# 512-column weight units over two row tiles in the second MLP products and the first half of the output projections of a diffusion trunk

## The chip, the cores and the metric

The kernel runs on one core of one Trainium2 chip. The core has TensorE (PE in the profile: matmuls, with a queue of its own for weight loads, PEld), VectorE (DVE), ScalarE (ACT), GpSimd (POOL) and SyncE (SP, which issues the DMAs here). The metric is the device time of one execution in microseconds (us); the figure for a kernel is the median of its runs. The profile comes from one profiled execution, and its times are counted from the start of that execution's span.

## The reference, cut to what matters

One inference step of a trunk of four layers, for 128 context tokens and 512 latent tokens with 1024 features each. Each layer has a token mixer (0 differential attention, 1 neighbourhood attention, 2 grouped-query attention, 3 a Hyena long convolution) and a squared-ReLU MLP, each with a residual, a LayerNorm and a modulation by a vector of conditions:

```python
for i in range(DEPTH):                                   # 4 layers
    mod_p = jnp.split((silu_ctx @ ada_w[i] + ada_b[i])[:, None, :], 6, axis=-1)
    mod_s = jnp.split((silu_c @ ada_w[i] + ada_b[i])[:, None, :], 6, axis=-1)
    hp, hs = modulate(xp, mod_p[0], mod_p[1]), modulate(xs, mod_s[0], mod_s[1])
    op, os_ = ...                                        # the mixer; its last step is  o @ w_o
    xp = layer_norm(DN_ALPHA * xp + mod_p[2] * op, ln_g[i, 0], ln_b[i, 0])
    xs = layer_norm(DN_ALPHA * xs + mod_s[2] * os_, ln_g[i, 0], ln_b[i, 0])
    fp = squared_relu_mlp(modulate(xp, mod_p[3], mod_p[4]), mlp_w1[i], mlp_w2[i])
    fs = squared_relu_mlp(modulate(xs, mod_s[3], mod_s[4]), mlp_w1[i], mlp_w2[i])
    xp = layer_norm(DN_ALPHA * xp + mod_p[5] * fp, ln_g[i, 1], ln_b[i, 1])
    xs = layer_norm(DN_ALPHA * xs + mod_s[5] * fs, ln_g[i, 1], ln_b[i, 1])

def squared_relu_mlp(h, w1, w2):                         # w1: 1024 x 4096, w2: 4096 x 1024
    return jnp.square(jax.nn.relu(h @ w1)) @ w2
```

The change concerns two products: `... @ w2` in the MLPs of layers 1, 2 and 3, and `o @ w_o` at the end of each mixer.

## The kernel before, in words

**Precision and tiles.** The 640 tokens are five row tiles of 128 (`NT` = 5; tile 0 is the context). Every product is made in split precision: each operand is held as a rounded part and a remainder, and `mm3` (L473) issues three matmuls for one product of 128x128 by some columns, at L475, L476 and L477. In the MLP's second product and in the output projection the 128x128 operand loaded into TensorE is an activation (`ff`, `oh`), and the columns streamed past it are those of a weight unit.

**Weight units.** Weights come from memory in units of 128x1024 elements, 512 KB, in the order of one list that `weight_order` (L346) writes. SP loads a unit into one of three `raw` buffers; `w_convert` (L436) makes the two parts of it in one of five `hl` buffers: a cast on ScalarE (L451), then a subtraction on VectorE (L453). `wget` (L463) hands the next unit of the list to the code and converts two more ahead (one, where `ahead=1`). A unit before the change (`unit_b`) holds four row blocks of the weight (the inner dimension, 4 x 128) by 256 columns.

**The MLP** (`mlp`, L864) runs through eight chunks of 512 inner features. For a chunk it makes the first product (`w1_unit`, 320 columns a matmul, rows with `hh` and `hl` as inputs), then the second product of the chunk before: four units `q`, and for each of them five row tiles in `w2_group` (L909), 12 matmuls of 256 columns into one PSUM tile named `w`. The tile comes from `any1` (L337), which takes four PSUM buffers in turn. Chunk 7's second product is made in `sublayer_end` and stays as it is.

**Evacuation.** `residual` (L649) takes the result off: a multiply by a gate on VectorE (L655, `gtmp`, three buffers) and an addition to the residual `r` (L662), on VectorE or GpSimd in a fixed ratio.

**Side work.** Between units `side` (L1543) works off what stands next in the list: steps of the next layer's modulation (adaLN; on VectorE, L543, with two loads on SP each, `adaw`), and in layers 0 to 2 the filters and their spectra for the Hyena mixer, whose DFT tables (`hyt`) stay in `hl` buffers while they are in use.

**The output projection** (`out_steps`, L825) has two halves of the inner dimension. The first half is a generator: 20 groups (four units by five tiles) that the mixer's end takes as filling work, each yield telling how much TensorE work it was; `out_rest` (L848) runs it down to 6 groups, prepares the second half in between, and takes the rest. `out_left` counts. The second half stays as it is.

Of the kernel before, what the change touches and what calls it, by code (L numbers as in the profile page):

```python
# [18 lines left out]
P = 128  # L19
# [10 lines left out]
DEPTH = 4  # L30
# [13 lines left out]
AHD = 1  # L44
OL0 = 20
OL1 = 6
WS = (0, 1, 2)
# [9 lines left out]
TSTEP = 3  # L57
LT = 3
CT = 4

# [138 lines left out]


def prepare(inp):
    g = {n: np.asarray(a) for n, a in inp.items()}
# [13 lines left out]
    d["w1"] = np.stack([np.stack([unit_a(g["mlp_w1"][l], np.arange(f * P, f * P + P)) for f in range(32)]) for l in range(DEPTH)])  # L216
    d["w2"] = np.stack([np.stack([unit_b(g["mlp_w2"][l], 4 * ch, q * 256) for ch in range(8) for q in range(4)]) for l in range(DEPTH)])
    for nm, wq, cf in (("da", g["da_w_qkv"][0], da_cols), ("na", g["na_w_qkv"][0], na_cols)):
# [7 lines left out]
    for nm, wo in (("da", g["da_w_o"][0]), ("na", g["na_w_o"][0]), ("gq", g["gq_w_o"][0][rows]), ("hy", g["hy_w_o"][0])):  # L226
        d[nm + "_o"] = np.stack([unit_b(wo, 4 * kh, q * 256) for kh in range(2) for q in range(4)])
    ck = g["cache_da_k"][0, 0].reshape(P, D)
# [51 lines left out]
class Trunk:  # L280
# [65 lines left out]
    def weight_order(self):  # L346
        out = []
        for n, l in enumerate(self.layers):
# [16 lines left out]
            for ch in range(9):  # L365
                for i in range(8):
                    if (ch < 8) if i < 4 else (ch > 0):
                        out.append(("w1", l, 4 * ch + i) if i < 4 else ("w2", l, 4 * ch + i - 8))
                        if 0 < ch < 8:
                            out += ada[:1] + side[i // 4].get(4 * (ch - 1) + i % 4, [])  # L370
                            ada = ada[1:]
        return out
# [270 lines left out]
    def restore(self):  # L643

        f, self.fetch_r = self.fetch_r, None
        if f:
            f()

    def residual(self, ps, t, q, quick=False):  # L649

# [169 lines left out]
    def out_first(self, l, nm, split):  # L820

        self.out_left = 4 * NT
        return self.out_steps(l, nm, split)

    def out_steps(self, l, nm, split):  # L825
        self.restore()
        self.load_gates(l, 0, (0,))
        gate = self.gate
        oh = self.out_half()
        self.w_convert(self.wi + 1)  # L830
        split(oh, 0, 0)
        split(oh, 0, 1)
        yield 1
        for q in range(4):
            u = {q: self.wget((nm + "_o", q), ahead=1)}
            if q == 1:
                self.load_gates(l, 0, (1,))
                gate.update(self.gate)
                self.gate = gate
            for t in range(NT):  # L840
                if q == 0 and t + 2 < NT:
                    split(oh, 0, t + 2)
                self.out_group(u, oh, t, (q,))
                self.out_left -= 1
                yield 1280
        self.scale_r = False

    def out_rest(self, l, nm, split, first):  # L848
        self.share = QW
        self.load_ln(l, 0)  # L850
        while self.out_left > 6:
            next(first)
# [11 lines left out]
    def mlp(self, l, nxt, last):  # L864
# [52 lines left out]
        for ch in range(8):  # L917
# [7 lines left out]
            for f in range(4):  # L925
                w1_unit(4 * ch + f)
                self.side()
            for q in range(4):
                u = self.wget(("w2", l, 4 * (ch - 1) + q))
                for t in range(NT):  # L930
                    w2_group(u, ch - 1, q, t)
                    groups += 1
                    if self.taps and groups % TSTEP == 0:
                        self.tap_step()
                self.side()
# [606 lines left out]

    def side(self):  # L1543

        while self.wlist[self.wi][0] in ("ada", "hyw", "hyt", "hyd", "hyc"):
            key = self.wlist[self.wi]
# [411 lines left out]
class Feeder:  # L1958
# [29 lines left out]
    def close(self):  # L1988
# [5 lines left out]
        self.debt += CRATE  # L1994
        while self.debt > 0 and self.k.out_left > 6:
            self.debt -= next(self.first)
# [237 lines left out]
```

## Time and profile before

| | us |
|---|---|
| median of three runs (lowest, highest) | 3492.54 (3490.21, 3494.48) |
| the profiled execution | 3491.57 |
| its span in the trace | 3489.7 |
| TensorE busy, 25288 matmuls | 3320.7 (95%) |
| TensorE's weight loads | 3187.3 (91%) |
| VectorE | 2603.5 (75%) |
| ScalarE | 1511.8 (43%) |
| GpSimd | 1010.7 (29%) |

In the chain of work that ended last TensorE has 57% of the span and VectorE 14%. The MLPs of layers 1, 2 and 3 lie at about 1300 to 1785, 2130 to 2617 and 3014 to 3480 us, the ends of the mixers, where the output projections run, at 337 to 444, 1208 to 1279, 2019 to 2116 and 2930 to 3001 us. Two things help in reading. Matmuls are pipelined, so the duration of one (0.28 us for 256 columns) overlaps the next; the rate is read from the distance between starts. And names in the trace leave the buffer's number out: `w` is the PSUM tile of an MLP product, `wo` that of an output projection, `hl` and `ff` are what it reads.

### The profile page before, as it was taken

How to read it: one execution, taken by the hardware profiler on the slowest of the kernel's cores; microseconds unless marked ns; L12 is line 12 of the kernel's file. 1: busy time of each engine (PE TensorE's matmuls, PEld its weight loads, DVE VectorE, ACT ScalarE, POOL GpSimd, SP SyncE). 2: the span in 40 equal slices, each digit the busy share in tenths (PEclk: the TensorE clock that was granted, in tenths of full speed). 3: DMA queues.
4: the chain of work that ended last, by engine and by line, in shares of the span. 5: the costliest groups of instructions: out<-in, count | busy, mean ns of one | idle time of the engine just before them, and what ended most of it. 6: DMA issues, size and time to landing. Idle time of an engine off the chain costs nothing.

```text
span 3489.7 us, 63708 instructions
## 1 busy us (share of the span) xinstructions
PE 3320.7 (95%) x25288; PEld 3187.3 (91%) x25288; DVE 2603.5 (75%) x4691; ACT 1511.8 (43%) x2700; POOL 1010.7 (29%) x961
## 2 busy tenths in 40 slices
PE   8999899999999989999988999999998999999998
PEld 6878899998999989999988889999998998899998
DVE  4777888788586678777677888787759888945457
ACT  4555453333356654433335665333424334432322
POOL 1323333334354453122252014232334112500002
PEclk9999999999999999999999999999999999999999
DMA  7333135545242324556412112545523224232221
GB/s 274 124 128 108 49 128 163 173 162 176 81 131 82 104 76 158 187 168 196 144 60 69 31 53 91 177 162 180 164 96 121 82 75 157 85 94 79 85 75 54
DMA packets 157643, 418.96 MB, mean 120 GB/s; under 512 B 19550, under 2 KB 29414, under 8 KB 154270
## 3 DMA queue, kind: packets, MB, share of 16 engines
q1 hardware_dynamic: 157344, 414.88, 36.3%
q8 instruction: 199, 3.26, 0.4%
q14 instruction: 100, 0.82, 0.1%
HBM read 371.20 MB, written 34.05 MB: 116 GB/s over the span
## 4 chain that ended last, share of the span: by engine, by line
PE 57%; DVE 14%; issue 2%; ACT 2%; DMA 2%; POOL 1%; SPq 0%; DVEq 0%; ACTq 0%; POOLq 0%
PE w L475 12%; PE w L476 12%; PE w L477 12%; DVE hl L453 2%; PE pv L2061 2%; PE s L2014 1%; PE qk L475 1%; PE ptp L1064 1%; DVE ada L543 1%; PE qk L477 1%; PE qk L476 1%; DVE gtmp L655 1%; DVE hl L736 1%; DVE r L662 1%; PE wo L477 1%
## 5 line engine op out<-in xcount | busy, mean ns | idle before, releaser
L662 POOL TENSOR_TENSOR r<-r,gtmp 128x256 f32<-128x256 f32 x444 | 437.7, 999 | 1125.6 <-DVE gtmp L655 1087.7
L453 DVE TENSOR_TENSOR hl<-raw,hl 128x1024 fp32r<-128x1024 f32 x390 | 508.7, 1307 | 317.6 <-ACT hl L451 316.2
L475 PE MATMUL w<-hl,ff 128*128 128x256 f32 x2560 | 715.6, 280 | 7.4 <-DVE gtmp L655 6.9
L476 PE MATMUL w<-hl,ff 128*128 128x256 f32 x2560 | 715.2, 279 | 2.5 <-DVE hl L453 2.4
L477 PE MATMUL w<-hl,ff 128*128 128x256 f32 x2560 | 714.0, 279 | 0.0
L451 ACT CAST hl<-raw 128x1024 fp32r<-128x1024 f32 x411 | 430.1, 1048 | 634.8 <-PE w L477 496.7
L475 PE MATMUL w<-hh,hl 128*128 128x320 f32 (+2 forms) x2048 | 637.2, 311 | 0.2
L476 PE MATMUL w<-hl,hl 128*128 128x320 f32 (+2 forms) x2048 | 634.4, 310 | 2.7 <-DVE hl L736 2.7
L477 PE MATMUL w<-hh,hl 128*128 128x320 f32 (+2 forms) x2048 | 634.0, 310 | 0.0
L475 PEld LDWEIGHTS w<-hl,ff 128*128 128x128 f32 x2560 | 481.2, 188 | 12.1 <-DVE gtmp L655 10.2
L476 PEld LDWEIGHTS w<-hl,ff 128*128 128x128 f32 x2560 | 481.5, 188 | 5.0 <-DVE hl L453 3.3
L477 PEld LDWEIGHTS w<-hl,ff 128*128 128x128 f32 x2560 | 480.3, 188 | 0.0
L543 DVE SCALAR_TENSOR_TENSOR ada<-adaw,sil,ada 128x512 f32<-128x512 f32 x504 | 388.7, 803 | 92.4 <-DMA adaw<-in_ada_w 75.5
L475 PEld LDWEIGHTS w<-hh,hl 128*128 128x128 f32 x2048 | 387.0, 189 | 13.8 <-issue 8.4
L476 PEld LDWEIGHTS w<-hl,hl 128*128 128x128 f32 x2048 | 386.7, 189 | 4.2 <-DVE hl L736 4.2
L477 PEld LDWEIGHTS w<-hh,hl 128*128 128x128 f32 x2048 | 386.5, 189 | 0.8 <-issue 0.8
L655 DVE TENSOR_TENSOR gtmp<-w,gate 128x256 f32<-128x256 f32 x640 | 261.6, 416 | 159.2 <-PE w L477 147.5
L874 ACT ACTIVATE fx<-w 128x640 f32<-128x640 f32 (+2 forms) x136 | 91.5, 672 | 453.8 <-PE w L477 446.4
L475 PE MATMUL qk<-hh,hl 128*128 128x320 f32 (+2 forms) x672 | 216.7, 322 | 6.7 <-DVE gtmp L655 3.9
L476 PE MATMUL qk<-hl,hl 128*128 128x320 f32 (+2 forms) x672 | 211.6, 315 | 1.3 <-DVE hl L736 1.3
L477 PE MATMUL qk<-hh,hl 128*128 128x320 f32 (+2 forms) x672 | 211.5, 315 | 0.0
L475 PE MATMUL wo<-hl,oh 128*128 128x256 f32 x640 | 184.1, 288 | 10.0 <-DVE gtmp L655 5.4
(344 smaller groups left out, 7135.4 us busy)
## 6 DMA issues: line engine op xcount, KB each, us to landing
raw<-in_w SPq DMA_DIRECT2D x256, 512.0 KB
adaw<-in_ada_w SPq DMA_DIRECT2D x288, 256.0 KB
adaw<-in_ada_w SPq DMA_DIRECT2D x16, 1024.0 KB
raw<-ab_d SPq DMA_DIRECT2D x32, 512.0 KB
raw<-in_hy_in SPq DMA_DIRECT2D x24, 512.0 KB
adaw<-in_ada_s SPq DMA_DIRECT2D x8, 1024.0 KB
raw<-in_da_qk SPq DMA_DIRECT2D x16, 512.0 KB
gate<-gate_d SPq DMA_DIRECT2D x32, 256.0 KB
```

Of the source, the lines that this page charges most:

```text
L451: self.nc.scalar.copy(t[:, 0], raw)
L453: sub(t[:, 1], raw, t[:, 0].bitcast(F32))
L475: mm(ps, w[0], x[0], start=start, stop=False)
L476: mm(ps, w[0], x[1], start=False, stop=False)
L477: mm(ps, w[1], x[0], start=False, stop=stop)
L543: nc.vector.scalar_tensor_tensor(out=y, in0=raw[h], scalar=x, in1=y, op0=ALU.mult, op1=ALU.add)
L655: nc.vector.tensor_mul(tmp, ps, self.gate[2 * s + q // 2][:, (q % 2) * 256:(q % 2) * 256 + 256])
L662: eng.tensor_add(rv, rv, tmp)
L736: self.last_dve = sub(self.hl[:, f, c], x, self.hh[:, f, c].bitcast(F32))
L874: nc.scalar.activation(x, src, AF.Relu)
L1064: nc.tensor.transpose(ps[:, i * P:(i + 1) * P], pr[:, (done + i) * P:(done + i + 1) * P], self.ident)
L2061: nc.tensor.matmul(ps[64 * h:64 * h + 64], self.v[:, self.chunk + c, vc:vc + 64], pts[h][:, c * P:(c + 1) * P], start=c == 0, stop=c == se ...
```

## The change

It concerns the second product of chunks 0 to 6 in the MLPs of layers 1 to 3 (`WIDE = 1`: layers from 1 on; the words "MLPs 2 to 4" count from one), and the first half of each of the four output projections.

A unit there is now two row blocks by 512 columns (`unit_w`), of the same 128x1024 elements. Two units make one half of the output columns. `wide_group` makes, for one row tile, 12 matmuls of 512 columns, six from each of the two units, into one PSUM tile of 128x2x256, and then calls `residual` twice, for its two halves of 256 columns. So for each chunk there are two halves by five tiles of wide groups in place of four units by five tiles of narrow ones. The code around it follows: the output projection counts 10 groups in place of 20 (thresholds 3 in place of 6, 2560 in place of 1280 a yield), loads the second half of its gates at the third tile, and takes two units before its first group. `side` is called after the third tile with half of what stands next in the list, and after the fifth with the rest; the list holds side work behind every second unit only.

```diff
-OL0 = 20
-OL1 = 6
+OL0 = 10
+OL1 = 3
+WIDE = 1
+def unit_w(w, k0, c0):
+    return w[k0 * P:(k0 + 2) * P, c0:c0 + 512].reshape(2, P, 512).transpose(1, 0, 2).reshape(P, 1024)
+def units_2(w, k0, wide):
+    if wide:
+        return [unit_w(w, k0 + 2 * kp, h * 512) for h in range(2) for kp in range(2)]
+    return [unit_b(w, k0, q * 256) for q in range(4)]
-    d["w2"] = np.stack([np.stack([unit_b(g["mlp_w2"][l], 4 * ch, q * 256) for ch in range(8) for q in range(4)]) for l in range(DEPTH)])
+    d["w2"] = np.stack([np.stack([u for ch in range(8) for u in units_2(g["mlp_w2"][l], 4 * ch, l >= WIDE and ch < 7)]) for l in range(DEPTH)])
-        d[nm + "_o"] = np.stack([unit_b(wo, 4 * kh, q * 256) for kh in range(2) for q in range(4)])
+        d[nm + "_o"] = np.stack([u for kh in range(2) for u in units_2(wo, 4 * kh, kh == 0)])
...
-                        if 0 < ch < 8:
-                            out += ada[:1] + side[i // 4].get(4 * (ch - 1) + i % 4, [])
-                            ada = ada[1:]
+                        wide = l >= WIDE and i > 3
+                        if 0 < ch < 8 and (not wide or i % 2):
+                            for n in range(4 * (ch - 1) + i % 4 - wide, 4 * (ch - 1) + i % 4 + 1):
+                                out += ada[:1] + side[i // 4].get(n, [])
+                                ada = ada[1:]
...
+    def wide_group(self, us, x, t, h):
+        c = slice(t * P, (t + 1) * P)
+        ps = self.any1([P, 2, 256], "w2")
+        for k in range(4):
+            u, f = us[k // 2], slice(k % 2 * 512, k % 2 * 512 + 512)
+            self.mm3(ps.rearrange("p a b -> p (a b)"), (x[:, 0, k, c], x[:, 1, k, c]), (u[:, 0, f], u[:, 1, f]), k == 0, k == 3)
+        for i in range(2):
+            self.residual(ps[:, i], t, 2 * h + i)
...
-        for q in range(4):
-            u = {q: self.wget((nm + "_o", q), ahead=1)}
-            if q == 1:
-                self.load_gates(l, 0, (1,))
+        for h in range(2):
+            us = [self.wget((nm + "_o", 2 * h + kp), ahead=1) for kp in range(2)]
             for t in range(NT):
-                if q == 0 and t + 2 < NT:
+                if h == 0 and t == 2:
+                    self.load_gates(l, 0, (1,))
...
-                self.out_group(u, oh, t, (q,))
+                self.wide_group(us, oh, t, h)
                 self.out_left -= 1
-                yield 1280
+                yield 2560
...
+            for h in range(2 if l >= WIDE else 0):
+                us = [self.wget(("w2", l, 4 * (ch - 1) + 2 * h + kp)) for kp in range(2)]
+                for t in range(NT):
+                    self.wide_group(us, ff[ch - 1], t, h)
+                    if t == 2:
+                        self.side(2)
+                self.side()
-            for q in range(4):
+            for q in range(0 if l >= WIDE else 4):
                 u = self.wget(("w2", l, 4 * (ch - 1) + q))
...
-    def side(self):
-        while self.wlist[self.wi][0] in ("ada", "hyw", "hyt", "hyd", "hyc"):
+    def side(self, parts=1):
+        n = 0
+        while self.wlist[self.wi + n][0] in ("ada", "hyw", "hyt", "hyd", "hyc"):
+            n += 1
+        for _ in range(-(-n // parts)):
```

The changed kernel's `mm3` stands at L489 to L491, its subtraction of a unit at L467, its gate multiply at L679, its residual addition at L686 and its adaLN step at L557.

TensorE's order in the MLP of layer 1, second product of the second chunk (`ff1`; its second and third unit before, its first and second half after). Before, where one unit ends and the next begins:

```order
L476 MATMUL w22104_16276<-hl222_16043,ff1_15033 128x256
L477 MATMUL w22104_16276<-hl222_16043,ff1_15033 128x256
L475 MATMUL w22106_16301<-hl224_16110,ff1_15033 128x256
L476 MATMUL w22106_16301<-hl224_16110,ff1_15033 128x256
L477 MATMUL w22106_16301<-hl224_16110,ff1_15033 128x256
```

After, where the first pair of units ends and the second begins:

```order
L491 MATMUL w22066_15814<-hl221_15653,ff1_14773 128x512
L489 MATMUL w22071_15851<-hl224_15716,ff1_14773 128x512
L490 MATMUL w22071_15851<-hl224_15716,ff1_14773 128x512
L491 MATMUL w22071_15851<-hl224_15716,ff1_14773 128x512
L489 MATMUL w22071_15851<-hl224_15716,ff1_14773 128x512
L490 MATMUL w22071_15851<-hl224_15716,ff1_14773 128x512
L491 MATMUL w22071_15851<-hl224_15716,ff1_14773 128x512
L489 MATMUL w22071_15851<-hl225_15729,ff1_14773 128x512
L489 MATMUL w22074_15870<-hl224_15716,ff1_14773 128x512
L490 MATMUL w22071_15851<-hl225_15729,ff1_14773 128x512
```

A group had its 12 matmuls from one unit; it now has six from the first unit of a pair (`hl224`) and six from the second (`hl225`).

VectorE's order at the same place, around the conversion (L453) of the unit that comes next but one. Before:

```order
L655 TENSOR_TENSOR gtmp2091_16180<-w22090_16167,gate1978_15027 128x256
L543 SCALAR_TENSOR_TENSOR ada2065_15879<-adaw2082_16115,sil_67,ada2065_15879 128x512
L662 TENSOR_TENSOR r1759_13552<-r1759_13552,gtmp2091_16180 128x256
L543 SCALAR_TENSOR_TENSOR ada2065_15879<-adaw2082_16115,sil_67,ada2065_15879 128x512
L655 TENSOR_TENSOR gtmp2093_16196<-w22092_16183,gate1978_15027 128x256
L543 SCALAR_TENSOR_TENSOR ada2065_15879<-adaw2083_16116,sil_67,ada2065_15879 128x512
L453 TENSOR_TENSOR hl226_16203<-raw226_16017,hl226_16203 128x1024
L655 TENSOR_TENSOR gtmp2097_16225<-w22096_16212,gate1977_15025 128x256
```

After, with the second unit of the next pair (`hl225`) and the first `w1` unit of the next chunk (`hl227`):

```order
L679 TENSOR_TENSOR gtmp2064_15808<-w22063_15795,gate1958_14767 128x256
L679 TENSOR_TENSOR gtmp2065_15811<-w22063_15795,gate1958_14767 128x256
L557 SCALAR_TENSOR_TENSOR ada2035_15489<-adaw2069_15842,sil_67,ada2035_15489 128x512
L686 TENSOR_TENSOR r1749_13422<-r1749_13422,gtmp2065_15811 128x256
L557 SCALAR_TENSOR_TENSOR ada2035_15489<-adaw2069_15842,sil_67,ada2035_15489 128x512
L467 TENSOR_TENSOR hl225_15729<-raw225_15627,hl225_15729 128x1024
L679 TENSOR_TENSOR gtmp2067_15827<-w22066_15814,gate1958_14767 128x256
L679 TENSOR_TENSOR gtmp2068_15830<-w22066_15814,gate1958_14767 128x256
L467 TENSOR_TENSOR hl227_15837<-raw227_15656,hl227_15837 128x1024
L679 TENSOR_TENSOR gtmp2072_15864<-w22071_15851,gate1959_14769 128x256
L679 TENSOR_TENSOR gtmp2073_15867<-w22071_15851,gate1959_14769 128x256
```

The multiplies of one PSUM tile (`w22063`, `w22066`, `w22071`) now stand in pairs, and the subtraction of a unit stands between two groups' pairs, directly ahead of the multiplies of the group that ends the first half.

## Rows read from the trace of the kernel before

**Rows 1.** The page's totals: busy us (share of span) x instructions.

```profile
PE 3320.7 (95%) x25288; PEld 3187.3 (91%) x25288; DVE 2603.5 (75%) x4691; ACT 1511.8 (43%) x2700; POOL 1010.7 (29%) x961
```

**Rows 2.** Windows: stretch, length, busy PE PEld DVE ACT POOL, PEclk, DMA share, GB/s.

```profile
1300.00:1785.00 485.00, 478.00 (x3634) 470.29 (x3633) 365.17 (x535) 184.91 (x249) 137.70 (x128) 0.99 0.49 162
3014.00:3480.00 466.00, 455.16 (x3476) 453.31 (x3474) 271.21 (x471) 142.40 (x191) 40.34 (x27) 0.99 0.25 77
```

**Rows 3.** PE's waits, MLPs of layers 1, 2, 3: total us, times, longest.

```profile
PE w L476 <- DVE hl L453: 2.4, 2, 1.3
...
PE w L475 <- DVE gtmp L655: 3.6, 5, 1.0
...
PE w L476 <- DVE hl L736: 1.0, 2, 0.7
```

**Rows 4.** PE's timeline, layer 3: first of 240 narrow matmuls, first behind them; twice.

```profile
3081.07 0.28 PE L475 MATMUL w<-hl,ff 128*128 128x256 f32 x1
...
3108.27 0.31 PE L475 MATMUL w<-hh,hl 128*128 128x320 f32 x1
...
3192.86 0.28 PE L475 MATMUL w<-hl,ff 128*128 128x256 f32 x1
...
3221.12 0.31 PE L475 MATMUL w<-hh,hl 128*128 128x320 f32 x1
```

**Rows 5.** Windows of 13.6 us, instructions of tile w alone (PE count first).

```profile
1488.80:1502.40 13.60, 13.60 (x122) 13.57 (x120) 2.82 (x7) 0.71 (x1) 1.00 0.35 109
3362.20:3375.80 13.60, 13.60 (x118) 13.60 (x116) 3.71 (x9) 0.70 (x1) 1.00 0.25 78
```

**Rows 6.** PE's timeline, layer 0: two pairs of 512 columns (L1585 and L1586).

```profile
532.65 0.40 PE L1585 MATMUL filt<-hl,hab 128*128 128x512 f32 x1
...
533.11 0.28 PE L475 MATMUL w<-hl,ff 128*128 128x256 f32 x1
...
541.89 0.40 PE L1585 MATMUL filt<-hl,hab 128*128 128x512 f32 x1
...
542.37 0.28 PE L475 MATMUL w<-hl,ff 128*128 128x256 f32 x1
```

**Rows 7.** PE's timeline: 320 columns (six apart), 384 columns (five apart, twice).

```profile
3062.01 0.31 PE L477 MATMUL w<-hh,hl 128*128 128x320 f32 x1
...
3062.89 0.31 PE L477 MATMUL w<-hh,hl 128*128 128x320 f32 x1
...
1321.98 0.34 PE L476 MATMUL w<-hl,hl 128*128 128x384 f32 x1
...
1322.85 0.34 PE L476 MATMUL w<-hl,hl 128*128 128x384 f32 x1
...
1316.08 0.34 PE L477 MATMUL w<-hh,hl 128*128 128x384 f32 x1
...
1316.96 0.34 PE L476 MATMUL w<-hl,hl 128*128 128x384 f32 x1
```

**Rows 8.** The page's groups: count | busy, mean ns | idle before, releaser.

```profile
L453 DVE TENSOR_TENSOR hl<-raw,hl 128x1024 fp32r<-128x1024 f32 x390 | 508.7, 1307 | 317.6 <-ACT hl L451 316.2
...
L451 ACT CAST hl<-raw 128x1024 fp32r<-128x1024 f32 x411 | 430.1, 1048 | 634.8 <-PE w L477 496.7
...
L655 DVE TENSOR_TENSOR gtmp<-w,gate 128x256 f32<-128x256 f32 x640 | 261.6, 416 | 159.2 <-PE w L477 147.5
```

**Rows 9.** Timeline, layer 1: a unit's cast, its subtraction, the matmul that waited.

```profile
1447.71 1.06 ACT L451 CAST hl<-raw 128x1024 fp32r<-128x1024 f32 x1 [6.32 <-PE w L477]
...
1450.48 3.09 DVE L453 TENSOR_TENSOR hl<-raw,hl 128x1024 fp32r<-128x1024 f32 x2
...
1451.95 0.39 PE L476 MATMUL w<-hl,ff 128*128 128x256 f32 x1 [1.29 <-DVE hl L453]
```

**Rows 10.** PE's waits at mixers' ends: layer 3, then layer 0.

```profile
PE wo L475 <- DVE gtmp L655: 4.8, 3, 2.9
...
PE pv L2206 <- DVE pt L1070: 3.7, 1, 3.7
```

More of the change, by code (lines that the diff above doesn't have):

```diff
@@ L820, in out_first @@
     def out_first(self, l, nm, split):
-        self.out_left = 4 * NT
+        self.out_left = 2 * NT
         return self.out_steps(l, nm, split)
@@ L833, in out_steps @@
         yield 1
-        for q in range(4):
-            u = {q: self.wget((nm + "_o", q), ahead=1)}
-            if q == 1:
-                self.load_gates(l, 0, (1,))
-                gate.update(self.gate)
-                self.gate = gate
-            for t in range(NT):
-                if q == 0 and t + 2 < NT:
+        for h in range(2):
+            us = [self.wget((nm + "_o", 2 * h + kp), ahead=1) for kp in range(2)]
+            for t in range(NT):
+                if h == 0 and t == 2:
+                    self.load_gates(l, 0, (1,))
+                    gate.update(self.gate)
+                    self.gate = gate
+                if h == 0 and t + 2 < NT:
                     split(oh, 0, t + 2)
-                self.out_group(u, oh, t, (q,))
+                self.wide_group(us, oh, t, h)
                 self.out_left -= 1
-                yield 1280
+                yield 2560
         self.scale_r = False
@@ L850, in out_rest @@
         self.load_ln(l, 0)
-        while self.out_left > 6:
+        while self.out_left > 3:
             next(first)
@@ L1994, in close @@
         self.debt += CRATE
-        while self.debt > 0 and self.k.out_left > 6:
+        while self.debt > 0 and self.k.out_left > 3:
             self.debt -= next(self.first)
```

## Prediction

> **What bounds the kernel now.** I read the page's totals first: TensorE is busy for 95% of the span and its weight loads for 91%, VectorE for 75% [rows 1]. Then the busy times by stage: in the MLPs of layers 1 and 3 TensorE is busy for 478.00 of 485 us and 455.16 of 466 us, at a granted clock of 0.99, the 2.4 GHz level [rows 2]. Then TensorE's waits in the three MLPs that the change touches: after their openings (which the change leaves alone) they come to 2.4 us in layer 1 and 3.6 us in layer 2, and the 1.0 us of layer 3 stand before its first wide product [rows 3]. So these stages end when the stream of matmuls ends. The question is what one matmul costs in that stream, which is the distance from its start to the next start; the duration printed in a row (0.28 us) is longer, because matmuls overlap.
>
> **Pitch of a narrow matmul.** Two unbroken runs of 240 matmuls of 256 columns show two values: 27.20 us / 240 = 113.3 ns, and 28.26 us / 240 = 117.75 ns [rows 4]. A run keeps its value until something interrupts it. I looked at 17 equal stretches of 13.6 us inside such runs in the three MLPs: 4 hold 122 or 123 matmuls (113.3 ns), 13 hold 116 to 118 (117.75 ns); one of each is shown [rows 5]. The mean of a pair of narrow matmuls is therefore (13 x 235.5 + 4 x 226.7) / 17 = 233.4 ns.
>
> **The change, part by part.**
>
> *Matmuls.* Three MLPs x 7 chunks x 2 halves x 5 row tiles x 12 = 2520 wide ones stand for 5040 narrow ones, and four output projections x 2 x 5 x 12 = 480 for 960. 3000 matmuls go, with 3000 weight loads; the columns streamed stay the same. What it brings is 3000 x (233.4 ns - pitch at 512 columns). That pitch has no long run in the trace. Four readings bound it. (a) The one 128x512 kind with the same operands, in pairs between narrow matmuls: 0.46 us for a pair at 532.65 and 0.48 us at 541.89 [rows 6], so 230 and 240 ns each, the change of width included. (b) Steady 320 columns: 0.88 us / 6 = 146.7 ns; 384: 0.87 / 5 = 174 ns, and in another run 0.88 / 5 = 176 ns [rows 7]. A line through 146.7 and 174 reaches 228.6 ns at 512. (c) The same rows per column: 384 runs at 0.453 to 0.458 ns a column, which makes 232 to 235 ns. (d) Twice the narrow pitch: 226.7 to 235.5 ns. I take 231 ns, between (b) and (c) and at the quicker pair of (a): 3000 x 2.4 = **7.3 us off**. Ends: 226.7 ns takes 20.1 us off, 235.5 ns adds 6.3, and the 240 ns of the slower pair would add 20.
>
> The Trainium skill (TensorE: Matmul & The Clock Gate, section Back-to-back issue gap) gives an isolated warm matmul N / 2.4 ns plus about 2.5 ns. By it a removed matmul is worth 2.5 ns and 3000 are worth 7.5 us. The trace does not follow its line: 256 columns should take 109 ns and 320 should take 136 ns, where the rows have 113.3 or 117.75 and 146.7 [rows 4, 7].
>
> *Evacuation.* Each wide group is read by two VectorE multiplies of the old shape (0.42 us each) and two adds, as two narrow groups were [rows 8]. No work is added, but both multiplies now come after the twelfth wide matmul. Four PSUM buffers take the groups in turn; each now holds 12 x 0.231 = 2.8 us of matmuls instead of 1.4. So VectorE may fall three groups, 8.3 us, behind before TensorE waits for a buffer, where it was 4.2. TensorE's five waits for these multiplies in layer 2's MLP, 3.6 us in all [rows 3], should go: **3.6 us off** (ends 3.6 and 0). Layer 3 has no such wait to lose.
>
> *Weight buffers.* Units keep their bytes: loads, ScalarE casts and VectorE subtractions (1.31 us each [rows 8]) are as many as before. But two units are now in use at once and come free together, out of five buffers, of which layer 1 keeps two and layer 2 one for DFT tables. While both tables are held, the pair leaves one buffer, so the second unit of the next pair is converted only when the old pair is done. The order shows this on TensorE and VectorE after the first half of the second chunk (its units 220 and 221 are followed by 224 and 225). The trace has such a release: the old unit's last matmul ends near 1447.7, the cast starts at 1447.71, and TensorE gets the converted unit at 1451.95, 4.2 us later, after VectorE has worked off other instructions [rows 9]. Without those it is cast plus subtraction, 1.05 + 1.31 = 2.4 us [rows 8]. Behind the waiting cast on ScalarE stand only later casts; behind the subtraction on VectorE stand the last group's evacuations, which have 8.3 us to spare. The cover on TensorE is the first unit's 6 matmuls and one or two more, 1.4 to 1.8 us, where 24 spectrum matmuls used to cover most of it. I count three such places in layer 1 (the first three pairs of halves) at 0.6 to 2.8 us, and take 1.2, since the order puts the subtraction at the head of VectorE's queue: 3.6 us, against the 2.4 us of the same wait already there [rows 3]. That is **1.2 us on** (ends 0 and 6). Layer 2 has one buffer more and layer 3 three more, so the next pair is ready there.
>
> *Side work.* The adaLN products are split in two parts per pair, after the third and the fifth row tile; their loads on SP stand two together instead of apart. The count is the same. A late load holds VectorE, and that is hidden by the doubled PSUM cover; if conversion of a unit is behind it, it costs TensorE what it costs now.
>
> *Output projections.* The first half's groups fill gaps at the end of each mixer. They come in pieces of 2.8 us instead of 1.4, need two converted units before the first group, and hold a PSUM buffer longer that the attention's transposes share. In the Hyena mixer three buffers are busy with the transforms, so the third unit cannot be converted while a pair is in use; four narrow groups that stood ahead of the last inverse transform become about one wide one there, and the rest runs afterwards. Against that, 4.8 us of waits for evacuation in this stretch may shrink, and 3.7 us of an attention wait in layer 0 may move either way [rows 10]. I take **0**, ends 5 off and 8 on.
>
> **Sum.** -7.3 - 3.6 + 1.2 + 0 = -9.7 us. The profiled execution took 3491.57 us (its span is 3489.7), so 3481.9; the median of the runs is 0.97 us higher, which makes the forecast **3483 us**. A difference under 0.2%, 7 us, cannot be told from no change in this kernel.
>
> **Rivals.**
>
> 1. *Columns, not matmuls, set the pace.* If the pitch stays at 233 to 235 ns for 512 columns, the wide form streams at the narrow one's rate and only the waits move. For it: 384 columns are no quicker per column than 256 [rows 4, 7]. Against it: (b). Time: 3000 x 0 to 2 ns on, 2.4 off for the waits: 3490 to 3496, say 3491. Chance 0.24.
>
> 2. *The pool of five weight buffers becomes the bound (slower).* Eight places in layer 1 (three changes of half, a fourth with a spectrum product, four ends of a chunk with one) pay the full 4.2 us less 1.4 us of cover, and eight in layer 2 pay 4.2 less 2.8: 8 x 2.8 + 8 x 1.4 = 33.6 us; with 7.3 off and 2.4 of the old waits gone, 3516. It decides the sign once these waits pass about 14 us in all. For it: rows 9 show the 4.2 us. Against it: the order has the conversion early on VectorE in most of these places. Chance 0.13. The Trainium skill (Perfetto Trace Analysis, section Optimization Strategy) says that a gap which keeps returning on the engine that should be full can mean too little room for the next tile; the wait in rows 9 agrees, twice in layer 1.
>
> 3. *Weight loads are the bound and halving them frees the stream.* Loads are busy for 91% of the span [rows 1]. The pitch would then fall to what the columns alone need, by the slope of (b) 0.427 x 512 = 218 ns: 3000 x 15.4 = 46 us off, 3444 with the waits. Against it: the pairs of rows 6 do not go under 230 ns. Chance 0.06. The Trainium skill (Perfetto Trace Analysis, section Identifying the Most-Contended Engine) judges headroom by the busy share of weight loads, which speaks for this rival; its gap of 215.8 ns at 512 columns would give 53 us off.
>
> 4. *The line (b) or the quicker narrow pitch holds.* 226.7 to 228.6 ns: 14 to 20 us off, with the waits 3469 to 3476. Chance 0.12.
>
> **How the numbers follow.** The forecast with its own spread (3476 to 3488) has 0.45. The range 3466 to 3499 takes in rivals 1 and 4 and leaves out rivals 2 and 3, 0.19. Faster by over 0.2%: 0.40 of the forecast's 0.45, rivals 3 and 4: 0.58. Within 0.2%: the other 0.05, and 0.22 of rival 1: 0.27. Slower: rival 2 and the rest of rival 1: 0.15.
>
> **What would show it.** Layer 3's MLP has neither side work nor buffer waits: its 7 chunks hold 840 wide matmuls, so a chunk's 120 should take 27.7 us (27.2 by rival 4, 28.3 by rival 1, 26.2 by rival 3). In layer 2's MLP the waits of TensorE for the multiplies should be gone. In layer 1's MLP TensorE should wait for the subtraction about three times for a microsecond each; many waits of 2 us or more there and in layer 2 are rival 2. I am wrong in the forecast if the chunk of layer 3 takes over 28 us, or if the mixers' ends lose more than 8 us.

## The result and the profile after

The changed kernel took 3532.45 us (3528.93 to 3544.28) against 3491.38 us for the kernel before: a ratio of 1.0123, 95% interval 1.0096 to 1.015. It is 41 us slower; 3483 was forecast, and 3499 was the upper end. The page's totals of the profiled execution (3535.88 us, span 3533.8):

```profile
PE 3333.9 (94%) x22288; PEld 3046.3 (86%) x22288; DVE 2603.4 (74%) x4691; ACT 1511.3 (43%) x2700; POOL 969.8 (27%) x961
```

Beside [rows 1]: 3000 matmuls and 3000 weight loads fewer, as counted, and TensorE busy 13 us longer. To see where, I cut each MLP from the last first-product matmul of its second chunk to that of its eighth; between them lie six whole chunks. The rows show the stretch, its length, and the busy time of PE, PEld, DVE, ACT and POOL, then the granted clock, the DMA share and GB/s. Before, layers 1, 2 and 3:

```profile
1360.30:1738.80 378.50, 375.97 (x2885) 368.76 (x2885) 287.84 (x424) 142.74 (x183) 99.31 (x92) 1.00 0.53 174
2196.20:2570.50 374.30, 370.28 (x2850) 362.38 (x2849) 281.93 (x420) 136.31 (x173) 105.61 (x92) 1.00 0.51 166
3080.90:3418.40 337.50, 337.50 (x2594) 337.50 (x2593) 173.53 (x312) 97.43 (x120) 0.00 (x0) 1.00 0.25 79
```

After:

```profile
1357.90:1761.60 403.70, 386.95 (x2167) 336.94 (x2166) 294.93 (x428) 142.79 (x183) 84.81 (x92) 0.99 0.51 164
2219.80:2617.10 397.30, 382.39 (x2130) 332.74 (x2130) 292.12 (x424) 136.27 (x173) 85.84 (x92) 0.98 0.49 158
3129.80:3463.60 333.80, 333.80 (x1875) 304.24 (x1874) 160.82 (x312) 97.45 (x120) 0.00 (x0) 1.00 0.26 79
```

Layer 3 gained 3.7 us. Layers 1 and 2 lost 25.2 and 23.0, and the rest of the span, taken as a sum, is the same within 0.5 us. That the rest comes out so even is luck: outside the MLP stretches, executions of these kernels differ by up to 12 us (see e7). Layers 1 and 2 are the ones with side work. TensorE's waits there (total, times, longest), layer 1 and then layer 2, against the first two rows of [rows 3]:

```profile
PE ada L562 <- DVE ada L557: 6.6, 4, 4.3
PE hs L490 <- DVE hl L467: 3.5, 2, 2.8
PE w L490 <- DVE hl L467: 3.4, 5, 1.6
PE adat L568 <- ACT adarow L565: 2.0, 1, 2.0
PE hs L489 <- ACT hl L465: 1.1, 1, 1.1
...
PE ada L562 <- DVE ada L557: 10.5, 5, 3.1
PE adat L568 <- ACT adarow L565: 3.9, 2, 1.9
PE w L489 <- DVE gtmp L679: 0.5, 1, 0.5
```

Of the 3.6 us of waits for the gate multiplies in layer 2, 0.5 is left; that they should go was forecast. New are waits of `ada` and `adat`. `ada<-ada,ones` is TensorE's own part of the side work: after eight adaLN steps (ScalarE does the first, VectorE adds up the others) one modulation vector stands in `ada`, and TensorE closes it with a product against ones, in four parts, then for most vectors transposes the row. The prediction never mentions that TensorE reads `ada`. The product's group in the layer 2 stretch (busy, mean ns | idle before), before and after:

```profile
L548 PE MATMUL ada<-ada,ones 128*32 128x512 f32 x48 | 6.4, 605 | 0.0
...
L562 PE MATMUL ada<-ada,ones 128*32 128x512 f32 x48 | 18.0, 721 | 10.5 <-DVE ada L557 10.5
```

The same 48 rows are spread over three times the time. Adding up the distances from each matmul's start to the next, waits taken off, gives the whole account (us):

| | layer 1 before, after | layer 2 before, after | layer 3 before, after |
|---|---|---|---|
| six chunks | 378.5, 403.7 | 374.3, 397.3 | 337.5, 333.8 |
| waits | 2.4, 16.7 | 3.6, 14.9 | 0, 0 |
| closing product, without its waits | 6.3, 15.7 | 6.0, 17.2 | none |
| first product | 169.6, 172.0 | 169.6, 172.3 | 169.0, 169.0 |
| second product | 171.0, 168.7 | 170.4, 167.8 | 168.5, 164.8 |
| spectra and the rest | 29.2, 30.6 | 24.7, 25.1 | none |

Here is one closing of six, the third vector of layer 2. Each of the four parts of the product has two rows on TensorE. Before, VectorE's four products of the last step (three rows of its timeline), then TensorE:

```profile
2350.31 0.75 DVE L543 SCALAR_TENSOR_TENSOR ada<-adaw,sil,ada 128x512 f32<-128x512 f32 x1 [3.40 <-DMA adaw<-in_ada_w]
...
2351.32 1.89 DVE L543 SCALAR_TENSOR_TENSOR ada<-adaw,sil,ada 128x512 f32<-128x512 f32 x2
...
2353.46 0.74 DVE L543 SCALAR_TENSOR_TENSOR ada<-adaw,sil,ada 128x512 f32<-128x512 f32 x1
...
2355.20 1.06 PE L548 MATMUL ada<-ada,ones 128*32 128x512 f32 x8
2356.19 0.42 PE L475 MATMUL w<-hh,hl 128*128 128x320 f32 x1
```

After, the same place, with TensorE's last row again the matmul behind the product:

```profile
2381.30 1.41 DVE L557 SCALAR_TENSOR_TENSOR ada<-adaw,sil,ada 128x512 f32<-128x512 f32 x2 [3.45 <-DMA adaw<-in_ada_w]
...
2383.30 1.19 DVE L557 SCALAR_TENSOR_TENSOR ada<-adaw,sil,ada 128x512 f32<-128x512 f32 x1
...
2384.74 0.74 DVE L557 SCALAR_TENSOR_TENSOR ada<-adaw,sil,ada 128x512 f32<-128x512 f32 x1
...
2386.07 2.89 DVE L557 SCALAR_TENSOR_TENSOR ada<-adaw,sil,ada 128x512 f32<-128x512 f32 x3
...
2389.55 1.16 DVE L557 SCALAR_TENSOR_TENSOR ada<-adaw,sil,ada 128x512 f32<-128x512 f32 x1
...
2383.77 0.40 PE L491 MATMUL w<-hl,ff 128*128 128x512 f32 x1
2387.32 3.53 PE L562 MATMUL ada<-ada,ones 128*32 128x512 f32 x6 [3.15 <-DVE ada L557]
...
2391.99 1.04 PE L562 MATMUL ada<-ada,ones 128*32 128x512 f32 x2
2392.97 0.41 PE L490 MATMUL w<-hl,hl 128*128 128x320 f32 x1
```

Before, the last load landed at 2350.3, only **one** step of four products came after it, and its sum ended at 2354.2, 1.0 us ahead of the closing product. After, the late landing holds **two** steps: eight products from 2381.30 to 2390.7, with multiplies in between, while TensorE was through with the half at about 2384. It waited 3.15 us, with first-product matmuls behind that need nothing of `ada`, and then its four parts no longer ran together but in three pieces: one part at 2387.32, two side by side at 2389.01, and the last at 2391.99, behind some first-product matmuls. A piece costs as much as all four parts together. When the whole sum is ready, eight rows start side by side and the next matmul follows 1.0 us later (2355.20 to 2356.19); the last part alone takes 0.98 us (2391.99 to 2392.97). The Trainium skill (TensorEngine Tiling (Array Packing), section Available Configurations) has the array work as four tiles in the 128x32 form. The `128*32` rows of before agree.

The first two pieces took longer still: six rows, 3.5 us, where two pieces of 0.98 us would make 2.0. The window shows why (fields as in the stretches above): behind the wait the granted clock was 0.50, the 1.2 GHz level.

```profile
2387.20:2390.60 3.40, 3.29 (x6) 0.36 (x6) 3.40 (x5) 0.00 (x0) 1.71 (x3) 0.50 0.00 0
```

So the row "closing product" holds two costs. By the starts in the trace the six products of each layer ran in fourteen pieces after, against seven (layer 1) and six (layer 2) before. Fourteen pieces of 0.98 us make 13.7 us; the 2.0 and 3.5 us above that are about half of the 4.3 and 7.4 us for which they ran at the lower clock.

SP's queue shows why two steps: the loads of the last step, before, then those of the last two steps, after (`adaw`, two loads a step).

```profile
2326.82 16.10 SPq L422 DMA_DIRECT2D raw<-in_w  x4
...
2344.17 1.64 SPq L432 DMA_DIRECT2D adaw<-in_ada_w  x2
```

```profile
2356.52 17.20 SPq L436 DMA_DIRECT2D raw<-in_w  x4
...
2374.97 2.89 SPq L446 DMA_DIRECT2D adaw<-in_ada_w  x4
```

In both kernels these loads are asked for when the second half of a chunk begins; here SP issues them 3.6 us into that half before and 5.0 us into it after. With two units taken at once, the step that used to be loaded one unit earlier is in that batch too.

One cost of a wait comes behind it. At 1666.41 TensorE had waited 2.03 us for `adarow`; the windows around it:

```profile
1664.00:1667.00 3.00, 0.97 (x8) 0.71 (x7) 3.00 (x5) 3.00 (x6) 0.00 (x0) 1.00 0.77 233
1667.00:1670.40 3.40, 3.40 (x15) 3.40 (x14) 0.31 (x3) 0.60 (x1) 0.00 (x0) 0.50 0.84 282
1670.40:1673.00 2.60, 2.60 (x20) 2.60 (x19) 0.00 (x0) 1.22 (x2) 0.00 (x0) 1.00 0.97 355
```

The granted clock was 0.50 for 3.4 us after it, and first-product matmuls stood 267 ns apart in place of 147. The trace of after has seven such stretches in the six chunks of layers 1 and 2, and the trace of before none. Those that fell on the first product are most of its 2.4 and 2.7 us.

### The profile page after: what moved, and what is told of

It is laid out like the page before. It is cut to its first block, busy times and chain, and to the rows that moved or that the text cites. A ratio compares the mean times of both kernels' runs of the same rounds, so it can differ in the third digit from the quotient of the medians.

```text
span 3533.8 us, 57574 instructions
## 1 busy us (share of the span) xinstructions
PE 3333.9 (94%) x22288; PEld 3046.3 (86%) x22288; DVE 2603.4 (74%) x4691; ACT 1511.3 (43%) x2700; POOL 969.8 (27%) x961
## 5 line engine op out<-in xcount | busy, mean ns | idle before, releaser
L467 DVE TENSOR_TENSOR hl<-raw,hl 128x1024 fp32r<-128x1024 f32 x390 | 506.6, 1301 | 438.3 <-ACT hl L465 428.0
L686 POOL TENSOR_TENSOR r<-r,gtmp 128x256 f32<-128x256 f32 x444 | 397.0, 908 | 1217.7 <-DVE gtmp L679 1205.9
L489 PE MATMUL w<-hh,hl 128*128 128x320 f32 (+2 forms) x2048 | 638.6, 312 | 1.2 <-ACT fx L898 1.0
L491 PE MATMUL w<-hh,hl 128*128 128x320 f32 (+2 forms) x2048 | 635.5, 310 | 0.0
L489 PE MATMUL w<-hl,ff 128*128 128x256 f32 (+1 forms) x1720 | 574.6, 334 | 6.2 <-DVE gtmp L679 6.2
L490 PE MATMUL w<-hl,ff 128*128 128x256 f32 (+1 forms) x1720 | 575.2, 334 | 3.5 <-DVE hl L467 3.4
L491 PE MATMUL w<-hl,ff 128*128 128x256 f32 (+1 forms) x1720 | 575.6, 335 | 0.0
L557 DVE SCALAR_TENSOR_TENSOR ada<-adaw,sil,ada 128x512 f32<-128x512 f32 x504 | 402.9, 838 | 70.5 <-DMA adaw<-in_ada_w 63.8
L489 PEld LDWEIGHTS w<-hh,hl 128*128 128x128 f32 x2048 | 388.1, 189 | 17.4 <-issue 7.9
L491 PEld LDWEIGHTS w<-hh,hl 128*128 128x128 f32 x2048 | 387.6, 189 | 1.7 <-issue 1.7
L489 PEld LDWEIGHTS w<-hl,ff 128*128 128x128 f32 x1720 | 322.9, 188 | 48.5 <-DVE gtmp L679 7.2
L679 DVE TENSOR_TENSOR gtmp<-w,gate 128x256 f32<-128x256 f32 x720 | 278.6, 414 | 112.4 <-PE w L491 102.0
L490 PEld LDWEIGHTS w<-hl,ff 128*128 128x128 f32 x1720 | 323.1, 188 | 43.6 <-DVE hl L467 7.4
L491 PEld LDWEIGHTS w<-hl,ff 128*128 128x128 f32 x1720 | 322.9, 188 | 37.0 <-issue 4.3
L489 PE MATMUL qk<-hh,hl 128*128 128x320 f32 (+2 forms) x672 | 217.4, 323 | 6.7 <-DVE gtmp L679 3.9
L491 PE MATMUL qk<-hh,hl 128*128 128x320 f32 (+2 forms) x672 | 212.0, 316 | 0.0
L686 DVE TENSOR_TENSOR r<-r,gtmp 128x256 f32<-128x256 f32 x336 | 173.7, 533 | 3.3
```

What stands on the lines that cost most here:

```text
L467: sub(t[:, 1], raw, t[:, 0].bitcast(F32))
L489: mm(ps, w[0], x[0], start=start, stop=False)
L490: mm(ps, w[0], x[1], start=False, stop=False)
L491: mm(ps, w[1], x[0], start=False, stop=stop)
L557: nc.vector.scalar_tensor_tensor(out=y, in0=raw[h], scalar=x, in1=y, op0=ALU.mult, op1=ALU.add)
L679: nc.vector.tensor_mul(tmp, ps, self.gate[2 * s + q // 2][:, (q % 2) * 256:(q % 2) * 256 + 256])
```

## The experiments

Theory A: the adaLN side work, late by one step, makes TensorE wait in order. Theory B: five weight buffers are too few for pairs (the second rival of the prediction). Theory C: wide matmuls or their evacuation cost by themselves. Times are medians; intervals are of the ratio to the kernel before.

**e1, pairs of narrow units.** The new frame with old matmuls:

```diff
-        ps = self.any1([P, 2, 256], "w2")
...
         for i in range(2):
...
+            ps = self.any1([P, 256], "w2")
...                                              # 12 matmuls of 256 columns from us[i]
```

> The changed kernel's frame (two units in use at once, side work behind every second unit and split in two, 10 groups in an output projection) with narrow matmuls: each group is two groups of 12 matmuls of 256 columns from one unit each. Theory A (side work: the loads of two adaLN steps come together and late, and TensorE waits in order for the product that closes a modulation vector): the pairing is what costs, so the time is that of the changed kernel, 3532, plus what the wide matmuls save, about 8: 3540 us. Theory B (the five weight buffers are too few for pairs): the same, 3540. Theory C (something in the wide matmuls or in their evacuation itself): about 3491, as before.

Measured: 3521.63 us, 1.0091 (1.0076 to 1.0106). The frame alone costs 31 us, so C is not the main cause. But I expected e1 8 us above the changed kernel, for what width saves, and it is 11 us below: with width the kernel is slower still, and layer 2 has 10.5 us of waits for `ada` where e1 has 4.8. In the third vector of layer 2, e1's loads landed 4.7 us ahead of the half's last matmul, the changed kernel's 2.5. Why they land later there no run settles. Layer 2 of e1 also has no stretch at a granted clock of 0.50, where the changed kernel has four of 3.4 us.

**e2, wide in layer 3 and the output projections only** (`WIDE = 3`).

> Wide units only in the MLP of layer 3 and in the output projections; layers 1 and 2 as before. Layer 3 has no side work and no DFT tables. Theories A and B: only the gain is left, 3.8 us in layer 3's chunks by the trace of the changed kernel, about 1 at its end and 2 at the mixers' ends: 3484 to 3487 us. Theory C: layer 3 and the output projections lose too, over 3495 us.

Measured: 3482.28 us, 0.9973 (0.9961 to 0.9984). Where there is no side work, the change gains time.

**e3, adaLN loads a unit earlier** in the changed kernel (`AAH = 2` becomes 3).

> The changed kernel with adaLN loads issued three weight units ahead in place of two, so that both loads of a pair are issued before the pair in front of them is worked off. Theory A: TensorE's waits for the closing product and its row (23 us in the MLPs of layers 1 and 2) go for the most part, with the low-clock stretches behind them: 3500 to 3510 us. Theory B: these waits are not the cause, 3528 to 3535 us.

Measured: 3489.51 us, 0.9997 (0.9985 to 1.0009); its ten runs lie between 3481.4 and 3496.4. One number takes back 43 us, some 8 more or less. Since units are taken in pairs, a unit earlier in the list means at the start of the half before. The 17 us of waits for `ada` are gone, and the closing product takes 6.0 and 7.8 us in the two stretches. I had put the gain too low since I priced the waits and the clock, and not the spread of the closing product. The waits for `hl` in layer 1 stay (8.2 us).

**e4, the closing product put off** to the next call of the side work, its transposes to the one after that:

```diff
-        if k < KD - 1:
-            return
+        if k == KD - 1:
+            self.closer = self.ada_close(l, m, acc)     # run by the next two calls of side()
...
+            yield                                       # ahead of the transposes
...
```

> The changed kernel with the closing product of each modulation vector put off to the next call of the side work (about a unit later), and its transposes to the one after that; loads stay where they are. Theory A: TensorE no longer stands in front of a product whose input is late; 3500 to 3510 us, with VectorE as late as before. If the late loads cost by holding VectorE's conversions of weights instead, TensorE's waits for hl grow by what the waits for ada lose: 3520 to 3532. Theory B: 3528 to 3535 us.

Measured: 3479.09 us, 0.9964 (0.9952 to 0.9977). That is 21 us under theory A's range. Loads and VectorE are as late as in the changed kernel (in the third vector of layer 2 the sum ends 6.5 us after the half's last matmul, there 6.7), so TensorE's place in line is what cost most. What the lateness still costs shows in e8: the closing product here takes 10.0 and 9.3 us in the two stretches.

**e5, the kernel before with loads a unit later** (`AAH = 2` becomes 1).

> The kernel before (narrow units, one at a time) with adaLN loads issued one weight unit ahead in place of two: nothing else is changed, so no pair, no wide matmul. Theory A (a late load makes TensorE wait in order for the product that closes a modulation vector): the same waits appear here, in the MLPs of layers 1 and 2 where the kernel before has none: 3510 to 3540 us. Theory B (buffers for weights): 3488 to 3494 us, nothing changes.

Measured: 3565.1 us, 1.0211 (1.0195 to 1.0227). This brings the loss out with no pair and no wide matmul, and more of it than I expected: the six chunks take 407.6 and 400.5 us in layers 1 and 2, against 378.5 and 374.3 before. Its waits in layers 1 and 2, the fifth vector of layer 2 on VectorE, and TensorE's closing product (one part, in 1.92 us; the granted clock was 0.50 there):

```profile
PE ada L548 <- DVE ada L543: 8.6, 6, 4.5
...
PE ada L548 <- DVE ada L543: 9.3, 4, 4.5
```

```profile
2548.39 0.75 DVE L543 SCALAR_TENSOR_TENSOR ada<-adaw,sil,ada 128x512 f32<-128x512 f32 x1 [5.01 <-DMA adaw<-in_ada_w]
...
2549.20 1.92 PE L548 MATMUL ada<-ada,ones 128*32 128x512 f32 x2 [4.48 <-DVE ada L543]
```

Layer 0 pays as well: its six chunks take 409.8 us, against 389.2 before.

**e6, the kernel before with e4's put-off closing product.**

> The kernel before with the closing product put off as in e4_close_later. Its MLPs of layers 1 and 2 have no waits for that product, its MLP of layer 0 has 5.5 us of them and spends 16.2 us on the products against 6. Theory A: layers 1 and 2 keep their time within 2 us and layer 0 gains up to 10: 3480 to 3488 us. So of the 11 us by which e4_close_later beat the kernel before, 5 to 8 would be layer 0's, and the wide units would be worth 3 to 6. If width is worth the whole 11: 3490.

Measured: 3486.66 us, 0.9987 (0.9977 to 0.9997). In the stretches only layer 0 gains (389.2 to 383.6 us in six chunks); layers 1 and 2 lose 1.9 and 1.3.

**e7, only the output projections wide** (`WIDE = 4`).

> Wide units in the first half of the output projections alone; all MLPs as before. The prediction put this at 0 with ends 5 off and 8 on; the traces of the changed kernel and of e2_layer3_only put the MLP of layer 3 at 3.7 us off, so this should be what is left of e2: 3486 to 3490 us. Over 3495 would mean that they lose and that layer 3 gained more than was read.

Measured: 3484.66 us, 0.9981 (0.9972 to 0.9991): 3 to 10 us gained where 0 was forecast. Outside the MLP stretches the profiled executions of these kernels differ by up to 12 us, so the traces do not say at which mixer: without the four MLP stretches e7's span is 2000.5 us against 2010.1 before, but e6, with narrow projections, has 2000.9.

**e8, both repairs** (e3 and e4) in the changed kernel.

> The changed kernel with both repairs: loads three units ahead (e3) and the closing product put off (e4). Theory A: with the product put off, the loads' lateness only holds VectorE, so little is left to gain: 3474 to 3482 us, waits for hl in layer 1 as in e3 and e4 (4 to 8 us). If VectorE's lateness still costs much, 3465 to 3473.

Measured: 3469.87 us, 0.9937 (0.9923 to 0.9952). This lies in the range that I gave for the case that VectorE's lateness still costs much: with the product put off, earlier loads gain 9 us more than e4. In the profiled executions the six chunks of layer 0 go from 383.8 to 377.6 us and those of layer 2 from 372.4 to 369.6. The closing product takes 6.0 us in layers 1 and 2, as before the change, with no waits. Left are, above all, waits for `hl`, in layer 1 and layer 2:

```profile
PE w L491 <- DVE hl L468: 7.8, 6, 2.3
PE hs L491 <- DVE hl L468: 0.7, 1, 0.7
...
PE w L491 <- DVE hl L468: 2.7, 3, 1.2
```

**e9, a table moved.** In e8, the second DFT table and the products that use it go from layer 1 to layer 2:

```diff
-                [{6 * i: x for i, x in enumerate(ctx)}, {3 * i: x for i, x in enumerate(dft[0])}],
-                [{}, {3 * i: x for i, x in enumerate(dft[1])}]][n] if n >= 0 else none
+                [{}, {3 * i: x for i, x in enumerate(dft[0])}],
+                [{6 * i: x for i, x in enumerate(ctx)}, {3 * i: x for i, x in enumerate(dft[1])}]][n] if n >= 0 else none
```

> e8_earlier_and_later with the spectra of the context's filters, and with them the second DFT table, moved from the MLP of layer 1 to that of layer 2; the work is the same. Layer 1 then holds one table in the five weight buffers, layer 2 two. Theory B for the waits for hl that are left (8.5 us in layer 1, 2.7 in layer 2): they change places, under 3 us in layer 1 and 7 to 9 in layer 2, total 3467 to 3473 us. If they come from VectorE's other work and not from the buffers, layer 1 keeps them.

Measured: 3471.7 us, 0.9949 (0.9934 to 0.9964). The waits change places with the table, layer 1 and layer 2:

```profile
PE w L491 <- DVE hl L468: 2.8, 3, 1.2
...
PE w L491 <- DVE hl L468: 7.5, 6, 2.1
```

So B is right for this part: one held table more, with the products that use it, costs about 6 us of waits with pairs. The products moved along with the table, so the run does not part the held buffer from their own work.

**e10, narrow units with both repairs.**

> The kernel before with both repairs of e8 (loads three units ahead, closing product put off), all units narrow. What e8 has over this is what width and pairing are worth once the side work is out of the way. By the traces: 3.7 us in layer 3, 2 to 5 each in the pitch of layers 1 and 2, less the waits for hl in layer 1, and 2 to 6 in the output projections: 3476 to 3483 us. If the repairs made the whole gain of e8: 3468 to 3472.

Measured: 3472.45 us, 0.9948 (0.9933 to 0.9963). That is just above the 3468 to 3472 that I gave for the case that the repairs made the whole gain of e8. The repairs alone are worth 18 us to the kernel before, and width over all three layers only some 3 more (e8), which the intervals do not tell from nothing. In six chunks e8 stands against it at 382.3 to 378.4 us in layer 1, 369.6 to 371.2 in layer 2 and 333.8 to 338.6 in layer 3.

**e11, both repairs, wide in layers 2 and 3** and the output projections, layer 1 narrow (`WIDE = 2`).

> e8 with layer 1's MLP narrow, wide units in layers 2 and 3 and in the output projections. If the pairs cost layer 1 more in waits for hl (8.5 us against 2.4) than the pitch gives it (2 to 4 us): 3465 to 3469 us. If width is worth more in layer 1 than it costs: 3471 to 3475.

Measured: **3460.81 us**, 0.9911 (0.9895 to 0.9928), the best version here, 30 us under the kernel before in the runs beside it, and 4 under the lower of my two ranges. It is 12 us quicker than e10, and the intervals of the two do not touch: with both repairs wide units do pay, but not in layer 1, whose six chunks take 377.9 us here and 382.3 in e8.

**e12, adaLN loads ahead of the weight loads of the same call** in the changed kernel (two lines exchanged).

> The changed kernel with one thing moved: each time a unit is taken, the adaLN loads that are due are issued ahead of the weight loads that are due, not behind them; how far ahead stays at two units. Theory A with SP's queue as the reason (the loads stand behind weight loads that wait for a buffer): most of the 40 us go, 3490 to 3505 us. If the loads are late because they are asked for too late in the program, whatever stands ahead of them: 3525 to 3535 us.

Measured: 3530.58 us, 1.0115 (1.0098 to 1.0132): no change. The test was weaker than I thought: in SP's queue the adaLN loads still come out behind four weight loads (17.2 us), those of earlier calls.

**e13 and e14, adaLN loads from GpSimd's and from ScalarE's queue** in the changed kernel.

> The changed kernel with the adaLN loads issued by GpSimd in place of SP, from the same calls. They then stand behind no weight load. If SP's queue makes them late (12.6 us of waiting weight loads ahead of them in the trace): they land up to 10 us earlier, the waits for ada in layers 1 and 2 fall from 17 us to under 5, 3490 to 3508 us. If the call comes too late in the program: 3525 to 3540 us. GpSimd's additions to the residual are held while it issues, which may take back a few us.

> The same from ScalarE's queue. There the casts of units stand ahead, and they wait for the release of a pair (9.3 us at 1697 to 1706.7 in the trace of the changed kernel), about as long as SP's weight loads wait. If what stands ahead in a queue is the reason: little or nothing is gained, 3515 to 3535 us, unlike from GpSimd. If e13 and this one are alike, SP's queue alone was the reason (both fast) or the call's place (both at 3530).

Measured: 3584.64 us, 1.026 (1.0241 to 1.0278), and 3553.32 us, 1.0167 (1.0145 to 1.0188). Neither helps; they are 52 and 21 us slower than the changed kernel, which I expected of neither. With GpSimd layer 0's six chunks alone take 425.1 us, against 388.9 after the change, and the waits for `ada` in layers 1 and 2 are longer than on SP:

```profile
PE ada L562 <- DVE ada L557: 11.8, 8, 2.2
...
PE ada L562 <- DVE ada L557: 13.0, 9, 2.3
```

This speaks against weight loads on SP as the whole reason, but GpSimd also has its additions in that queue, so the share of SP's queue stays open. The Trainium skill (Trainium Kernel Development and Optimization, section Key Constraints) has all these queues feed the same DMA engines, another issuer saving only issue time. That neither run gained agrees with it; why both lost it does not say, and no run here settles it.

**e15, side work in one piece** after the fifth row tile.

> The changed kernel with the side work of a pair done in one piece after its fifth row tile, not in two after the third and the fifth. The loads stay as late. Theory A: VectorE then does both steps, eight products of 0.74 us, after the end of the half, so TensorE waits longer for the closing product: 3535 to 3560 us. If the split itself were the cost: 3490 to 3515 us.

Measured: 3532.75 us, 1.0119 (1.0102 to 1.0136), the time of the changed kernel and under theory A's range (3535 to 3560). The split is no cause. It is no help either: in the closing shown above the loads for the first part land after the third tile.

## Why the prediction was wrong, point by point

- **Side work: the step that failed.** The prediction said of the paired loads that "the count is the same" and that "a late load holds VectorE, and that is hidden by the doubled PSUM cover". The cover protects the evacuation of groups. It does not protect a product of TensorE that reads what VectorE sums, and TensorE takes its work in order. I asked what stands behind the wait on VectorE, not who reads `ada`. Neither of the signs of being wrong that the prediction named would have shown it: the chunk of layer 3 took 27.46 us, and what lies outside the MLP stretches lost nothing. In layers 1 and 2 waits for `ada` and `adarow` (8.6 and 14.4 us), the spread of the closing product (9.4 and 11.2) and the slower first product (2.4 and 2.7) make 48.7 us. Of the spread, about 15 us are the pieces and about 5.5 the lower clock (an estimate, from the 0.98 us of a piece). e3, e4 and e5 show it from three sides. The kernel before had it in view: 1.0 us of margin in the closing above, and in layer 0's MLP, where the closing product takes 16.2 us, the wait itself:

```profile
PE ada L548 <- DVE ada L543: 5.5, 6, 1.4
```

- **Pitch: right mechanism, size too small.** In layer 3 the 120 wide matmuls of a chunk should take 27.7 us. Two rows of after, the first of them and the first matmul behind them:

```profile
3129.96 0.39 PE L489 MATMUL w<-hl,ff 128*128 128x512 f32 x1
...
3157.42 0.31 PE L489 MATMUL w<-hh,hl 128*128 128x320 f32 x1
```

  27.46 us / 120 = 228.8 ns, at the line of reading (b) (228.6, the fourth rival's), where I took 231. In the six-chunk stretches the 2160 wide matmuls brought 2.3, 2.6 and 3.7 us, 8.6 in all, where 2160 x 2.4 ns = 5.2 was forecast. Layer 3 refutes the first rival (columns set the pace). The third (weight loads) falls too: PEld went from 91% to 86% of the span, and the pitch stayed above its 218 ns.
- **PSUM cover: right.** Layer 2's 3.6 us of waits [rows 3] are 0.5.
- **Weight buffers: right mechanism, too small.** 1.2 us on was forecast, with 6 as its end; layer 1's waits for a unit went from 2.4 to 8.0 us, 5.6 on. The end held, the value did not: I counted three places, the trace of after has eight. e9 shows that these waits go with the second table and its products.
- **Output projections: too cautious.** 0 was forecast; e7 gained 3 to 10 us, beyond the end of 5 off in part of its interval.
- **Sum.** 48.7 from the side work, 5.6 from weight buffers, 3.1 off for the PSUM cover, 8.6 off for the pitch and 1.8 for the spectra and the rest make 44.4 us on, the growth of the three stretches; the two profiled spans differ by 44.1. The output projections are not in this sum: their gain of e7 does not show in these two executions. Forecast were 9.7 off.
- **The slower rival.** It had the sign but not the mechanism. Its 34 us of waits for converted units are 8.0 us in layer 1 and none in layer 2; the time came from a wait that no rival named.

## What to carry to other kernels

When a change regroups work, follow every step of the side work to its last reader, above all to one on the engine that bounds: a product that stands in line there turns a late input of another engine into its own idle time. Read the margin of such joins in the profile (here 1.0 us, between a sum's end and the product that reads it) before calling a delay hidden, and count how many steps stand behind the last load to land. Such a product can often be put off by one call, and its loads asked for one unit earlier; here the two were worth 18 us to the kernel before. Without them wide units paid only where there was no side work; with them the best version (e11) has wide units in layers 2 and 3 and in the projections, and layer 1 narrow.

## What the runs showed of the hardware

- Undisturbed, 512 columns take 228.8 ns from start to start and 256 columns 117.0 on average (168.5 us / 1440 in layer 3), so a wide matmul saves 5.2 ns against two narrow ones, a little over 2%. Runs of narrow matmuls kept one of two values, 113.3 or 117.75 ns; the six runs of 120 wide ones in layer 3 all kept 228.8 to 228.9.
- Four products in the 128x32 form run side by side when their inputs are all there (eight rows, and 1.0 us to the next matmul); one of them alone takes as long (0.98 us), so four that come in three pieces cost three times as much.
- At about the end of waits of 2.03 and 3.15 us the granted clock fell to 0.50, and it was there for 3.4 us. Behind the first this cost 1.8 us again (15 matmuls at 267 ns in place of 147); behind the second it stretched two pieces of the closing product from 2.0 to 3.5 us.
